# A two-layer diffusion backbone: weight splits moved from GpSimd and VectorE to VectorE and ScalarE, the second layer's shift and scale as packed matmuls

## The chip, the cores and the metric

The kernel runs on one core of a Trainium2 chip. The metric is the device time of one execution in microseconds; the time given for a kernel is the median of its timed runs. TensorE's clock has two levels, 1.2 and 2.4 GHz; the profile gives the mean of what was granted in a stretch as a fraction of the full one.

## What is computed

Two layers over 512 latent and 256 context tokens, width 2048, float32. Each layer: RMS norm, shift and scale by a modulation vector, a token mixer, and a gated residual. Layer 0's mixer is a bidirectional gated linear recurrence (16 blocks of 128 channels), layer 1's is differential attention with 16 heads.

```python
for i in range(2):
    shift, scale, gate = split(silu(c) @ mod_w[i] + mod_b[i], 3)          # for latent; the same with c_ctx
    h = rms_norm(x, norm_g[i]) * (1 + scale) + shift                      # latent and context tokens
    if i == 0:
        u, g = split(h @ lru_w_in, 2)
        xc = depthwise_conv(u) + conv_b
        r, ig = sigmoid(block_matmul(xc, gate_w) + gate_b)                # per direction
        y = (scan_forward + scan_backward)(r, ig, xc) * silu(g) @ lru_w_out
    else:
        q, k, v, g = split(h @ att_w_in, 4)                               # q, k: norm and rotary positions
        o = (softmax(q1 @ k1.T) - lam * softmax(q2 @ k2.T)) @ v           # per head
        y = (rms_norm(o) * silu(g)) @ att_w_out
    x = x + gate * y
return x                                                                  # latent tokens
```

## The kernel before

Every large product runs as three matmuls in a reduced-precision float32 form: an operand is *split* into a high part (a cast) and the rest (a subtraction), and high x high, high x low and low x high are summed in PSUM. Weights come in units of 128 x 1024 (512 KB), loaded on SP's queue into two buffers `raw`, split by `weights` into `wh` and `wl` (five buffers each; in layer 1 every sixth unit goes to an extra one). `split` (lines 43 to 50) issues the cast on one engine (line 49, or 47 on ScalarE) and the subtraction on another (line 50). The default is a cast on VectorE and a subtraction on GpSimd; in the attention every second unit is subtracted on VectorE, and the first output columns of the attention are cast on ScalarE. A unit's `raw` buffer is free for the next load when both are done.

The program runs in stages. The *prologue* loads and transposes the tokens and computes layer 0's shift and scale from 64 units of `mod_w`: four k-tiles of 256 columns go as four matmuls with 32-column stationary operands into the four quarters of PSUM's partitions (line 295), and `mod_cols` adds the four quarters with a small matmul (line 148). The *projections* (`phase1`) run 32 half-blocks (`proj`: 96 matmuls of 384 columns, lines 327 to 331), less the three begun in the prologue; between them, for each of 16 blocks, `padded` and `lru_conv` (first tap on GpSimd, line 426, three on VectorE, line 428, then the split into xh and xl), `lru_block` (24 gate matmuls of 386 columns, lines 451 to 453, ScalarE's functions, VectorE's scans) and `lru_out`. All of it shares eight PSUM banks. Beside it runs `mod_stream`, layer 1's shift and scale: `proj` takes a step of it after each weight unit (64/42 on average, from the eleventh unit on). A step loads a unit of 512 KB and adds it on VectorE, four multiply-adds of 512 columns (line 102); every eighth step's sums go through 16 small matmuls (line 115). The *output product* (`phase2`) multiplies by `w_out` in four column chunks of 512 (lines 557 to 559, three matmuls for each of six token tiles and two k-tiles of a unit; the fourth chunk in two halves), beside it layer 0's gate by VectorE's multiply-adds (line 102) and one matmul with ones (line 522); behind the last chunk the rows are normed and transposed again (`h_evac`: a product on ScalarE, a split). The *attention* (`phase3`, `head`) has, for each head, projections of 256 columns (lines 692 to 694), and between them the scores, softmax and products of the head before; `qk_norm` takes the four rotary products of q and of k on GpSimd (line 715). `early_out` and `phase4` are the attention's output product.

The order on each engine is the compiler's: it simulates the program as written, and issues by priority what is ready in the simulation. The engines then run their lists in order. `issue_after` keeps an instruction behind a named one on its own engine; `mod_stream` uses it to keep its steps behind the last result of `lru_out` (`self.mark`).

Of the kernel before, what the change touches and what calls it, by code (L numbers as in the profile page):

```python
# [29 lines left out]
# the last head's attention and the units of the first output columns beside it ("."), in order:  # L30
# q: channels, s: scores, t: transposes, v: times v, o: back to rows, f: norm, y: output
# [5 lines left out]
class Kern:  # L37
# [5 lines left out]
    def split(self, raw, hi, lo, hi_eng, lo_eng):  # L43
        """raw (float32) == hi + lo, both float32r"""
        nc = self.nc
        if hi_eng is nc.scalar:
            nc.scalar.copy(hi, raw)  # L47
        else:
            hi_eng.tensor_copy(hi, raw)  # L49
        return lo_eng.tensor_tensor(lo, raw, hi.bitcast(F32), op=ALU.subtract)  # L50

    def weights(self, src, shape, hi_eng=None, lo_eng=None):
        """one weight unit [128, 1024] from DRAM, split in two"""
# [10 lines left out]
        self.split(raw, h, l, hi_eng or nc.vector, lo_eng or nc.gpsimd)  # L64
# [9 lines left out]
    def rsqrt(self, pool, v, n, pre, bufs=1):  # L74
        """v ** -0.5 of a small tile: a guess from the bits of v, then Newton's steps"""
# [12 lines left out]
    def mod_vec(self, ch, pool, nm, bufs=1):  # L88
        """512 columns of silu(c) @ mod_w: sums over the channel tiles, one per partition"""
# [18 lines left out]
    def mod_stream(self, pool, chunks):  # L108
        """shift and scale of layer 1: four channel tiles per chunk"""
        nc = self.nc  # L110
        def sums(ch, acc):
            ps = self.psum("mcol")
            for s in range(4):
                for m in range(2):
                    nc.tensor.matmul(ps[:, 4 * s + 2 * m:4 * s + 2 * m + 2], acc[m][:, 128 * s:128 * s + 128],
                                     self.ones[:, 0:2], start=True, stop=True)
            for s in range(4):
                self.mod_col(1, 4 * ch + s, ps[:, 4 * s:4 * s + 4:2])

        last = None  # L120
# [22 lines left out]
    def mod_cols(self, layer, part, ch):  # L143
        """sums of the partials, channel-major: [128 channels, (latent, context)] x 2"""
# [97 lines left out]
    def rows(self, t, unit):  # L242
        """rms rows of one token tile, transposed"""
# [30 lines left out]
    def pairs(self, pool, unit):  # L274
        """shift and scale of layer 0 for two channel tiles at a time; behind them, h of these
        tiles and their part of the first three half-blocks"""
# [9 lines left out]
        for n in range(65):  # L286
            p, ch = n // 8, n // 8 + 8 * (n // 4 % 2)
            if n < 64:
# [3 lines left out]
                w = unit().rearrange("p (k c) -> p k c", k=4)  # L292
                nc.sync.dma_start(w, a["mod_w"][ch, u])
                for j in range(4):
# [829 lines left out]
```

## Time and profile before

| | |
|---|---|
| timed runs (median of 3) | 2505.36 us (2503.09 to 2505.61) |
| span of the profiled execution | 2499.5 us |
| TensorE busy, matmuls | 2350.4 us (94%), 15744 |
| TensorE busy, weight loads | 2197.3 us (88%) |
| VectorE busy | 1875.8 us (75%), 3292 instructions |
| ScalarE busy | 858.5 us (34%), 1826 |
| GpSimd busy | 694.9 us (28%), 390 |
| loads and stores | 298.83 MB, mean 120 GB/s |

The span runs from the first to the last instruction of one profiled execution; the timed runs take in what lies around it. In the rows below PE is TensorE (PEld its weight loads), DVE VectorE, ACT ScalarE, POOL GpSimd and SP the queue that issues most loads; L50 is line 50 of the code. Matmuls are pipelined, so TensorE's busy time is the time in which at least one was under way, and the pitch is read from the starts of successive ones. A float32 matmul that isn't in the reduced form leaves two records.

### The profile page before, as it was taken

What the parts mean: (1) busy time and instruction counts of PE and PEld (TensorE: products, weight loads), DVE (VectorE), ACT (ScalarE), POOL (GpSimd) and SP (SyncE); (2) the same over time, 40 slices, a digit from 0 to 9 for tenths busy, and PEclk for the clock granted to TensorE, in tenths of its full rate; (3) what the DMA queues carried; (4) which work ended last, traced back from release to release, by engine and by line L of the source; (5) the groups of instructions that cost most, each with busy time, mean ns of one, the idle gap of its engine ahead of it and who ended that gap; (6) DMA issues with size and microseconds to landing.
All of it is one profiled execution on the core that took longest, in us unless ns stands there. A gap on an engine that the chain in (4) does not pass through costs nothing.

```text
span 2499.5 us, 39647 instructions
## 1 busy us (share of the span) xinstructions
PE 2350.4 (94%) x15744; PEld 2197.3 (88%) x15744; DVE 1875.8 (75%) x3292; ACT 858.5 (34%) x1826; POOL 694.9 (28%) x390
## 2 busy tenths in 40 slices
PE   5989998989889899799999999999999999998899
PEld 4679998989889788679999999999999999997687
DVE  6457999999997866786787777778677766767622
ACT  4346535435337100033333333333333333235400
POOL 1243343433332233333121111212121211211352
PEclk8999999999999999999999999999999999999999
DMA  9912344434333655431232232322222211213552
GB/s 355 364 60 89 125 127 135 133 125 135 129 122 108 232 191 176 144 119 58 70 97 65 89 98 62 92 81 85 89 81 89 80 52 57 68 43 115 181 184 76
DMA packets 106473, 298.83 MB, mean 120 GB/s; under 512 B 12320, under 2 KB 33072, under 8 KB 106288
## 3 DMA queue, kind: packets, MB, share of 16 engines
q1 hardware_dynamic: 101536, 287.33, 35.2%
q10 hardware_dynamic: 4752, 8.98, 1.0%
q8 instruction: 123, 2.02, 0.3%
q14 instruction: 62, 0.51, 0.1%
HBM read 277.45 MB, written 18.82 MB: 119 GB/s over the span
## 4 chain that ended last, share of the span: by engine, by line
PE 42%; DVE 9%; DMA 3%; issue 2%; ACT 1%; POOL 1%; SPq 0%; DVEq 0%; ACTq 0%; POOLq 0%
PE pj L694 9%; PE pj L693 9%; PE pj L692 9%; PE sc L755 3%; PE acc L557 2%; DVE wh L49 2%; PE acc L558 2%; PE acc L559 2%; PE atr L778 1%; DMA raw<-w_kv 1%; DVE wl L50 1%; DMA raw<-w_o 1%; PE o L792 1%; PE o L791 1%; PE o L790 1%
## 5 line engine op out<-in xcount | busy, mean ns | idle before, releaser
L50 POOL TENSOR_TENSOR wl<-raw,wh 128x1024 fp32r<-128x1024 f32 x202 | 533.8, 2643 | 1334.8 <-DVE wh L49 975.1
L692 PE MATMUL pj<-wh,h 128*128 128x256 f32 x2560 | 730.2, 285 | 3.3 <-DVE v L50 2.7
L694 PE MATMUL pj<-wh,h 128*128 128x256 f32 x2560 | 729.2, 285 | 0.2
L693 PE MATMUL pj<-wl,h 128*128 128x256 f32 x2560 | 729.1, 285 | 0.0
L692 PEld LDWEIGHTS pj<-wh,h 128*128 128x128 f32 x2560 | 489.9, 191 | 6.2 <-DVE v L50 2.9
L693 PEld LDWEIGHTS pj<-wl,h 128*128 128x128 f32 x2560 | 490.2, 192 | 4.5 <-issue 2.6
L694 PEld LDWEIGHTS pj<-wh,h 128*128 128x128 f32 x2560 | 490.2, 191 | 3.1 <-issue 0.4
L49 DVE CAST wh<-raw 128x1024 fp32r<-128x1024 f32 x256 | 212.6, 832 | 173.4 <-PE acc L559 82.0
L102 DVE SCALAR_TENSOR_TENSOR ma<-mw,scT,ma 128x512 f32<-128x512 f32 x360 | 310.5, 906 | 18.9 <-DMA mw<-mod_v 18.9
L327 PE MATMUL proj<-h,wh 128*128 128x384 f32 x1024 | 265.5, 340 | 6.9 <-DVE h L49 6.9
L329 PE MATMUL proj<-h,wh 128*128 128x384 f32 x1024 | 271.6, 337 | 0.0
L331 PE MATMUL proj<-h,wl 128*128 128x384 f32 x1024 | 270.4, 336 | 0.0
L327 PEld LDWEIGHTS proj<-h,wh 128*128 128x128 f32 x1024 | 185.5, 190 | 15.2 <-DVE h L49 11.1
L329 PEld LDWEIGHTS proj<-h,wh 128*128 128x128 f32 x1024 | 187.2, 189 | 4.2 <-issue 2.0
L331 PEld LDWEIGHTS proj<-h,wl 128*128 128x128 f32 x1024 | 186.9, 189 | 0.8 <-issue 0.8
L761 ACT ACTIVATE p<-sc,mx 128x768 f32<-128x768 f32 x128 | 114.5, 904 | 113.1 <-DVE mx L757 108.1
L557 PE MATMUL acc<-wh,h 128*128 128x512 f32 x384 | 152.4, 398 | 0.0
L757 DVE TENSOR_REDUCE mx<-sc 128x2 f32<-128x1536 f32 x64 | 112.1, 1752 | 52.5 <-PE sc L755 52.3
L558 PE MATMUL acc<-wl,h 128*128 128x512 f32 x384 | 150.4, 392 | 0.1
L559 PE MATMUL acc<-wh,h 128*128 128x512 f32 x384 | 149.8, 391 | 0.0
L47 ACT CAST athl<-atr 128x512 fp32r<-128x512 f32 (+1 forms) x128 | 55.7, 483 | 196.7 <-PE atr L778 196.5
L755 PE MATMUL sc<-k,q 128*128 128x512 f32 (+1 forms) x512 | 108.2, 339 | 2.5 <-ACT p L761 2.5
(241 smaller groups left out, 3942.8 us busy)
## 6 DMA issues: line engine op xcount, KB each, us to landing
mw<-mod_v SPq DMA_DIRECT2D x96, 512.0 KB, 3.8
mw<-mod_w SPq DMA_DIRECT2D x64, 512.0 KB, 9.8
raw<-w_in SPq DMA_DIRECT2D x64, 512.0 KB, 3.6
raw<-w_kv SPq DMA_DIRECT2D x64, 512.0 KB, 3.7
raw<-w_qg SPq DMA_DIRECT2D x64, 512.0 KB, 3.9
raw<-w_out SPq DMA_DIRECT2D x40, 512.0 KB, 4.3
raw<-w_o SPq DMA_DIRECT2D x40, 512.0 KB, 3.5
raw<-mod_v SPq DMA_DIRECT2D x64, 256.0 KB, 3.6
```

Source lines behind the costliest of these rows:

```text
L49: hi_eng.tensor_copy(hi, raw)
L50: return lo_eng.tensor_tensor(lo, raw, hi.bitcast(F32), op=ALU.subtract)
L102: nc.vector.scalar_tensor_tensor(acc[m], w[:, k, :], sc, acc[m], op0=ALU.mult, op1=ALU.add)
L327: nc.tensor.matmul(ps[g][:, :384], wh, h[g][:, 0, :], start=first, stop=False)
L329: nc.tensor.matmul(ps[g][:, :384], wh, h[g][:, 1, :], start=False, stop=False)
L331: nc.tensor.matmul(ps[g][:, :384], wl, h[g][:, 0, :], start=False, stop=last)
L557: nc.tensor.matmul(acc[t], yh, wh, start=(kt == first), stop=False)
L558: nc.tensor.matmul(acc[t], yh, wl, start=False, stop=False)
L559: nc.tensor.matmul(acc[t], yl, wh, start=False, stop=(kt == last))
L692: nc.tensor.matmul(ps, h[:, 0, c], wh, start=(kt == 0), stop=False)
L693: nc.tensor.matmul(ps, h[:, 0, c], wl, start=False, stop=False)
L694: nc.tensor.matmul(ps, h[:, 1, c], wh, start=False, stop=(kt == KT - 1))
```

## The change

`weights` has no choice of engines any more: every weight unit is cast on ScalarE and subtracted on VectorE. The gate weights of `lru_block` go the same way; the first tap of the convolution goes to ScalarE; the subtractions of `h_evac` and the rotary products of `qk_norm` go to VectorE. What stays on GpSimd are clearings and, once, the tables of the rotary positions.

Layer 1's shift and scale are computed as layer 0's were: 16 chunks of four units, four packed matmuls for each unit, a copy of the partial sums on ScalarE and `mod_cols`. A step of `mod_stream` multiplies the unit loaded one step earlier and issues the next one's load, with no `issue_after`. The number of loads (64 of 512 KB) is unchanged, and so are the steps' places in `proj`. The host's layout of `mod_w` and `mod_v` follows, as do the chunk numbers in `mod_gate` and `gate_rows`.

```diff
-    def weights(self, src, shape, hi_eng=None, lo_eng=None):
+    def weights(self, src, shape):
...
-        self.split(raw, h, l, hi_eng or nc.vector, lo_eng or nc.gpsimd)
+        self.split(raw, h, l, nc.scalar, nc.vector)
...
-    def mod_stream(self, pool, chunks):
...
-        for ch in chunks:
-            g = self.mod_vec(4 + ch, pool, 2, 2)
-            for u in range(8):
-                with self.tc.issue_after(self.mark.ins) if self.mark else nullcontext():
-                    next(g)
-                yield
-                if u == 3 and last:
-                    sums(*last)
-            last = ch, self.macc
-        sums(*last)
+    def mod_unit(self, layer, ch, u, mps, w):
+        for j in range(4):
+            self.nc.tensor.matmul(mps[32 * j:32 * j + 32, :256], self.scp[:, 4 * u + j, :], w[:, j, :],
+                                  start=(u == 0), stop=(u == 3), tile_position=(0, 32 * j))
+    def mod_load(self, layer, ch, u, w):
+        w = w.rearrange("p (k c) -> p k c", k=4)
+        self.nc.sync.dma_start(w, self.a["mod_w"][layer, ch, u])
+        return w
+    def mod_part(self, mps, pool):
+        part = pool.tile([128, 256], F32, tag="mpart", bufs=2, name="mpart")
+        self.nc.scalar.copy(part, mps[:, :256])
+        return part
+    def mod_stream(self, pool):
+        unit = lambda n: self.mod_load(1, n // 4, n % 4, pool.tile([128, 1024], F32, tag="mw", bufs=2, name="mw"))
+        w, sums = unit(0), None
+        yield
+        for n in range(64):
+            ch, u = n // 4, n % 4
+            if u == 0:
+                mps = self.psum("mps")
+            self.mod_unit(1, ch, u, mps, w)
+            if n < 63:
+                w = unit(n + 1)
+            if u == 1 and sums:
+                self.mod_cols(1, *sums)
+            if u == 3:
+                sums = self.mod_part(mps, pool), ch
+            yield
+        self.mod_cols(1, *sums)
...
-        self.split(t, h[:, 0, :], h[:, 1, :], nc.vector, nc.gpsimd if g and kt % 2 == 0 else nc.vector)
+        self.split(t, h[:, 0, :], h[:, 1, :], nc.vector, nc.vector)
...
-        nc.gpsimd.tensor_scalar(xc, u[:, 2:2 + UL], cw[:, b, 2:3], self.convb[:, b:b + 1], op0=ALU.mult, op1=ALU.add)
+        nc.scalar.activation(xc, u[:, 2:2 + UL], AF.Identity, scale=cw[:, b, 2:3], bias=self.convb[:, b:b + 1])
...
-            self.split(raw, *self.gates, nc.vector, nc.gpsimd)
+            self.split(raw, *self.gates, nc.scalar, nc.vector)
...
-                nc.gpsimd.tensor_tensor(tv[:, :, c, :, h, :], xv[:, 0:4, c, :, 1 - h, :], sv[:, :, :, h, :], op=ALU.mult)
+                nc.vector.tensor_tensor(tv[:, :, c, :, h, :], xv[:, 0:4, c, :, 1 - h, :], sv[:, :, :, h, :], op=ALU.mult)
```

## Rows read from the trace of the kernel before

**Rows 1.** Table of stretches: busy us and instructions (x) per engine, clock, load share

```profile
150.00:802.00 652.00, 595.27 (x3306) 587.83 (x3305) 599.26 (x697) 322.57 (x434) 246.07 (x97) 0.95 0.37 121
802.00:1118.00 316.00, 292.60 (x1312) 238.32 (x1311) 245.85 (x329) 48.14 (x101) 106.59 (x41) 0.96 0.54 174
1118.00:2270.00 1152.00, 1132.52 (x9206) 1112.24 (x9205) 849.03 (x1784) 383.44 (x1069) 235.32 (x194) 1.00 0.24 75
2270.00:2420.00 150.00, 136.09 (x647) 110.56 (x646) 87.24 (x159) 47.24 (x103) 53.86 (x26) 0.95 0.54 174
2420.00:2499.50 79.50, 74.60 (x330) 61.43 (x328) 18.77 (x25) 0.00 (x0) 23.88 (x10) 0.98 0.28 89
```

**Rows 2.** Timeline, TensorE, projections: start us, us, instructions merged

```profile
480.56 0.51 PE L327 MATMUL proj<-h,wh 128*128 128x384 f32 x2
...
481.60 0.51 PE L327 MATMUL proj<-h,wh 128*128 128x384 f32 x2
```

**Rows 3.** Table of stretches, by tile: PE, PEld and others of proj; mcol; ma

```profile
150.00:802.00 652.00, 494.47 (x2793) 487.69 (x2791) 15.19 (x30) 27.97 (x78) 0.95 0.37 121
150.00:802.00 652.00, 14.73 (x128) 15.40 (x128) 5.12 (x32) 0.95 0.37 121
150.00:802.00 652.00, 14.73 (x128) 15.40 (x128) 211.11 (x256) 0.95 0.37 121
```

**Rows 4.** TensorE's waits in the projections: us in total, times, longest

```profile
PE gps L451 <- DVE xh L49: 32.1, 9, 7.8
PE gps L452 <- DVE xl L50: 17.0, 12, 2.5
PE gps L451 <- DVE ab L141: 3.8, 1, 3.8
PE gps L451 <- ACT r L455: 3.8, 1, 3.8
```

**Rows 5.** TensorE's waits in the output product, longest

```profile
PE gps L522 <- DVE ma L102: 20.0, 2, 13.2
```

**Rows 6.** Groups by form, whole span: busy us, mean ns, idle before, releaser

```profile
L50 POOL TENSOR_TENSOR wl<-raw,wh 128x1024 fp32r<-128x1024 f32 x202 | 533.8, 2643 | 1334.8 <-DVE wh L49 975.1 <-DVE l L762 72.6 <-ACT wh L47 47.4
L102 DVE SCALAR_TENSOR_TENSOR ma<-mw,scT,ma 128x512 f32<-128x512 f32 x360 | 310.5, 906 | 18.9 <-DMA mw<-mod_v 18.9
L49 DVE CAST wh<-raw 128x1024 fp32r<-128x1024 f32 x256 | 212.6, 832 | 173.4 <-PE acc L559 82.0 <-DMA raw<-w_o 25.6 <-DMA raw<-w_qg 25.0
L50 DVE TENSOR_TENSOR wl<-raw,wh 128x1024 fp32r<-128x1024 f32 x70 | 100.2, 1431 | 7.1 <-ACT wh L47 6.1
L1007 DVE SCALAR_TENSOR_TENSOR g<-g,pj 128x128 f32<-128x128 f32 x64 | 18.0, 282 | 10.6 <-ACT g L1006 9.9
L47 ACT CAST wh<-raw 128x1024 fp32r<-128x1024 f32 x16 | 16.8, 1050 | 16.9 <-DMA raw<-w_o 15.4 <-POOL rt L715 1.4
```

**Rows 7.** Timelines of VectorE and GpSimd, four places, in order of time

```profile
565.59 5.38 DVE L102 SCALAR_TENSOR_TENSOR ma<-mw,scT,ma 128x512 f32<-128x512 f32 x8
...
1051.12 6.13 POOL L50 TENSOR_TENSOR wl<-raw,wh 128x1024 fp32r<-128x1024 f32 x2 [4.54 <-DVE wh L49]
1052.94 6.18 DVE L102 SCALAR_TENSOR_TENSOR ma<-mw,scT,ma 128x512 f32<-128x512 f32 x4 [0.63 <-DMA mw<-mod_v]
...
2309.20 1.22 DVE L50 TENSOR_TENSOR wl<-raw,wh 128x1024 fp32r<-128x1024 f32 x1
```

**Rows 8.** Timeline, TensorE, prologue: packed products and small sums between projections

```profile
100.77 1.50 PE L295 MATMUL mps<-mw,scp 128*32 128x256 f32 x24
...
106.28 0.34 PE L331 MATMUL proj<-h,wl 128*128 128x384 f32 x1
106.55 0.64 PE L295 MATMUL mps<-mw,scp 128*32 128x256 f32 x8
107.12 0.98 PE L327 MATMUL proj<-h,wh 128*128 128x384 f32 x4
...
111.18 0.50 PE L148 MATMUL mcol<-sel,mpart 128*128 128x2 f32 x4
111.54 0.60 PE L327 MATMUL proj<-h,wh 128*128 128x384 f32 x2
```

More of the change, by code (lines that the diff above doesn't have):

```diff
@@ L106, in mod_vec @@
         yield
-    def mod_stream(self, pool, chunks):
[L110 to L120, printed above, removed]
-        for ch in chunks:
-            g = self.mod_vec(4 + ch, pool, 2, 2)
-            for u in range(8):
-                with self.tc.issue_after(self.mark.ins) if self.mark else nullcontext():
-                    next(g)
-                yield
-                if u == 3 and last:
-                    sums(*last)
-            last = ch, self.macc
-        sums(*last)
+    def mod_unit(self, layer, ch, u, mps, w):
[27 more added lines that the diff above has]
+        self.mod_cols(1, *sums)
     def mod_col(self, layer, c, src):
@@ L291, in pairs @@
                     mps = self.psum("mps")
-                w = unit().rearrange("p (k c) -> p k c", k=4)
-                nc.sync.dma_start(w, a["mod_w"][ch, u])
-                for j in range(4):
-                    nc.tensor.matmul(mps[32 * j:32 * j + 32, :256], self.scp[:, 4 * u + j, :], w[:, j, :],
-                                     start=(u == 0), stop=(u == 3), tile_position=(0, 32 * j))
+                self.mod_unit(0, ch, u, mps, self.mod_load(0, ch, u, unit()))
                 if n % 32 == 4:
@@ L314, in pairs @@
             if n % 4 == 3:
-                part = pool.tile([128, 256], F32, tag="mpart", bufs=2, name="mpart")
-                nc.scalar.copy(part, mps[:, :256])
-                sums = part, ch
+                sums = self.mod_part(mps, pool), ch
         for t in todo:
@@ L353, in phase1 @@
                 nc.gpsimd.memset(x, 0.0)
-            self.stream, self.slots = self.mod_stream(pool, range(8)), -16
+            self.stream, self.slots = self.mod_stream(pool), -16
             gates = lambda b: self.lru_block(b, x[b], pool)
@@ L516, in mod_gate @@
         nc = self.nc
-        yield from self.mod_vec(12 * layer + n, pool, nm)
+        yield from self.mod_vec(n, pool, nm)
         gt = self.gt[n] = pool.tile([128, nm, 512], F32, tag="gt", bufs=gbufs, name="gt")
@@ L534, in gate_rows @@
                 for i in range(2):
[L535 removed]
+                    nc.sync.dma_start(w[:, i], a["mod_v"][4 + n // 2, u + i][:, :, c])
                 for k in range(4):
@@ L875, in early_out @@
                     self.yload(u)
-                w = self.weights(a["w_o"][0, u], (2, 512), nc.scalar, nc.vector if u % 2 else None)
+                w = self.weights(a["w_o"][0, u], (2, 512))
                 with self.tc.issue_after(self.after.ins) if self.after else nullcontext():
@@ L958, in head @@
             return None
-        w = [self.weights(a["w_kv"][hd, u], (4, 256), None, nc.vector if u % 2 and hd else None) for u in range(4)]
+        w = [self.weights(a["w_kv"][hd, u], (4, 256)) for u in range(4)]
         if first:
@@ L1001, in head @@
         st["so"] = pa.tile([128, 4], F32, tag="so", bufs=2, name="so")
-        w = [self.weights(a["w_qg"][hd, u], (4, 256), None, nc.vector if u % 2 else None) for u in range(4)]
+        w = [self.weights(a["w_qg"][hd, u], (4, 256)) for u in range(4)]
         for t in range(4):
@@ L1073, in layout @@
     o["cT"] = c(np.stack([f["c"][0], f["c_ctx"]], -1).reshape(16, 128, 2).transpose(1, 0, 2))
-    o["mod_w"] = c(f["mod_w"][0, :, :4096].reshape(4, 4, 128, 16, 256).transpose(3, 0, 2, 1, 4))
-    v = f["mod_w"].transpose(1, 0, 2).reshape(2048, 12288)[:, 4096:]
-    o["mod_v"] = c(v.reshape(8, 2, 128, 16, 512).transpose(3, 0, 2, 1, 4))
+    o["mod_w"] = c(f["mod_w"][:, :, :4096].reshape(2, 4, 4, 128, 16, 256).transpose(0, 4, 1, 3, 2, 5))
+    v = f["mod_w"][:, :, 4096:].transpose(1, 0, 2).reshape(2048, 4096)
+    o["mod_v"] = c(v.reshape(8, 2, 128, 8, 512).transpose(3, 0, 2, 1, 4))
     o["mod_bT"] = c(f["mod_b"][:, :4096].reshape(2, 32, 128).transpose(2, 0, 1))
```

1 line of the change is left out of this document (removed).

## The prediction

> **What bounds the kernel now.** I cut the span where the work changes and read each stretch by the table of stretches [rows 1]: the prologue (0 to 150 us), the projections of layer 0 (150 to 802), their output product (802 to 1118), the attention heads (1118 to 2270) and the last output product. TensorE is busy everywhere, so the question in each stretch is what TensorE would need by itself, and who holds it up for the rest.
>
> In the projections VectorE is busy 599.26 of 652 us and TensorE 595.27 [rows 1]. TensorE's own need comes from its pitch at full clock: six 384-column matmuls start in 1.04 us (480.56 to 481.60), 0.1735 us each [rows 2]. 2793 projection matmuls lie in the stretch [rows 3]; the 16 x 24 gate matmuls of the code have 386 columns, so 0.1744 us each; the 128 small sums take 14.7 us [rows 3]: 484.6 + 67.0 + 14.7 = 566 us. So 86 of 652 us are lost: 56.7 idle (652 - 595.27), the rest in slices at 1.2 GHz, which the mean granted clock of 0.95 shows [rows 1]. The list of waits names the cause: 49.1 us of that idle time are gate matmuls waiting for VectorE's split of the convolution (xh, xl) [rows 4]. VectorE is the limit of this stretch, and TensorE stands close behind it.
>
> In the output product TensorE misses 23.4 us (316 - 292.60), 20.0 of them in two waits for the last multiply-add of the gate [rows 1, 5]; the clock then falls to its lower level. In the attention only 19.5 of 1152 us are idle at clock 1.00 [rows 1]: TensorE is the bound there and nothing this change touches can give much. After 2270 it misses 13.9 + 4.9 us.
>
> GpSimd's part is in the same rows. One of its splits takes 2643 ns on average [rows 6], and VectorE instructions that meet one grow: eight multiply-adds take 5.38 us (0.67 each) where it rests, but four take 6.18 us beside two GpSimd splits of 6.13 us [rows 7]. On average a multiply-add takes 906 ns [rows 6].
>
> **The change, part by part.** (1) *The second layer's shift and scale.* 256 VectorE operations (211.1 us in the projections [rows 3]) go, and 128 small sums on TensorE (14.7 us [rows 3]). In come 64 units of 4 packed products (8 records each). One between two projections moved the next one from 106.28 + 0.17 to 107.12, so it costs 0.67 us [rows 8]; three in a row take 1.50 us, 0.50 each [rows 8]. I take 0.67, as the stream hands out about one unit per weight unit: 64 x 0.67 = 43 us, bounds 32 to 43 at full clock, 86 if all fell into slices at half clock. The sums are now 16 groups of 4 small matmuls, each holding TensorE for 0.36 us (111.18 to 111.54 [rows 8]): 6 us. Sixteen copies on ScalarE lie beside. Net on TensorE: 43 + 6 - 14.7 = +34 us.
>
> The Trainium skill (TensorEngine Tiling (Array Packing), Key Properties) says that changing the tiling mode drains the TensorE. The row bears this out in kind, as a lone unit costs 0.17 us more than one in a row; if every unit cost only what one in a row does, the sum would be 11 us lower.
>
> The 64 loads stay as many and as large (512 KB). They are no longer placed behind the mixer's mark; each is issued on SP's queue right after the unit before it, some 8 us ahead of its use. A late load used to delay VectorE; now it would block TensorE, with all projections queued behind. I cost that at nothing, because TensorE's list of waits in this stretch has two more entries of 3.8 us each and neither is a load; the bounds are 0 and the 18.9 us that VectorE's multiply-adds of both streams waited for such loads [rows 6].
>
> (2) *The splits.* All 256 weight casts on VectorE (832 ns [rows 6]) go to ScalarE, where the 16 casts already there took 1050 ns [rows 6]; the 202 subtractions on GpSimd go to VectorE at 1431 ns as measured among GpSimd's, or 1.22 us alone [rows 6, 7]. In the projections that is 58 units (and 8 gate weights): VectorE loses 55 us and gains 66 x 1.22 = 81; ScalarE gains 66 x 1.05 = 69 us, and at most 16 x 1.05 = 17 for the convolution's first tap, which has fewer columns. VectorE there: 599 - 211 - 55 + 81 = 414 us before any relief from GpSimd's disappearance; ScalarE: 323 + 69 + 17 and 16 small copies, each shorter than such a cast (at most 17), = 426. Both are far below TensorE's need.
>
> (3) *Projections, sum.* TensorE needs 566 + 34 = 600 us. VectorE at 414 no longer holds the gates back, so the 49 us of waits and most of the low-clock slices behind them go. What is late next is ScalarE (table loads, gate functions and now the casts in one queue) and the eight PSUM banks, of which one is now held by a running sum for four units. I leave 12 us for these: 612 against 652, -40 us. Bounds: -50 (hardly anything left over) to -10 (loads and banks hold TensorE).
>
> (4) *Output product.* 40 casts leave VectorE (33 us at the mean), 40 subtractions come (49 us alone), 8 subtractions of h (384 columns) as well, its 128 multiply-adds stay. From 1052.94 to 1059.12 four of them took 6.18 instead of 2.7 us [rows 7], right ahead of the end of the 13.2 us wait [rows 5]. Each of the two GpSimd splits there cost VectorE about (6.18 - 2.7) / 2 = 1.7 us; for the eight weight units of that half chunk that is 14 us, and the dearer subtractions give 8 x (1.22 - 0.83) = 3 back. So some 10 of the 13 us go, the other wait (6.8 us) likewise in half, and with them the low-clock time: -20 us, bounds -30 to 0.
>
> (5) *Attention.* Per head VectorE loses 8 casts (6.7 us), gains about 4 subtractions (4.9) and 8 rotary products of 128 columns, at about 282 ns, the row of like size [rows 6] (2.3 us): even. ScalarE gains 8 x 1.05 = 8.4 us in about 72. These stand in queues that carry the softmax: a cast ahead of an exponential delays the transposes behind it by up to 1.05 us. TensorE has projection matmuls beside, placed by the compiler's schedule, and ScalarE's share goes from 383/1152 to about 517/1152 [rows 1]. I cost it at 0, bounds -10 (half the idle time) to +40 (2.5 us per head, two of eight casts exposed and one subtraction part-way).
>
> (6) *Ends.* In the last output product the chain load, cast, split shortens by 2.64 - 1.22 = 1.4 us [rows 6, 7] at each unit that GpSimd split, though ScalarE's cast is 0.2 slower: -5 us, bounds -10 to +2. The prologue's own work stays, and its six weight units have over 100 us of its loads to hide in: 0, bounds +-3.
>
> **How the numbers follow.** -40 - 20 + 0 - 5 = -65 us. The profiled span is 2499.5 us; the median of the three timed runs, 2505.36, stands 5.9 us above it, and I carry that over: 2499.5 - 65 + 5.9 = 2440 us.
>
> **Rivals.** *More is freed*: the waits of all stages go (-50, -30, -10, -10): 2405 us. For it: VectorE's waits alone explain most of TensorE's idle time. Against: each stage has a second limit close by. 0.14.
>
> *TensorE waits for the stream*: loads, banks or ScalarE's copies hold it in the projections, (3) gives -15 and the rest as forecast or a little less: 2465 to 2480. For it: SP's queue is one line, shared by weights whose buffers now wait for two busy engines. 0.18.
>
> *Slower, by the attention*: casts and subtractions stand ahead of the softmax on ScalarE and VectorE, and TensorE, which now idles 19.5 us, waits in every head. It decides once more than 65 us are lost there, 4.1 us per head out of the 13.3 us moved into these queues; at 6 us per head, 2536 us. Against: VectorE's load is even and ScalarE stays under half. 0.09.
>
> *It does not do what it says, or cancels*: the schedule packs differently and the 34 us of added TensorE time eat what the waits return in the projections (0), the attention loses what the output product wins: about 2502 us. 0.04.
>
> Forecast 0.55. The range 2408 to 2484 leaves out about half of the best case and the two worst, 0.2 in all. About 0.2% (5 us) is what a measurement of this kernel can tell from no change; faster 0.87, same 0.04, slower 0.09.
>
> **What would show it.** After: no GpSimd splits; VectorE near 60% in the projections; the multiply-adds of the gate near 0.67 us each; the waits for xh and xl gone; about 43 us of packed products between projections; the projections ending near 762 instead of 802; the wait of the gate's product under 5 us; an idle time in the attention still near 20 us. It would be wrong if TensorE's waits for the stream's loads or for ScalarE's evacuations exceed 25 us in the projections, or if the attention stretch grows beyond 1190 us.

## The result, and the profile of the kernel after

The kernel after takes 2441.84 us (median of 4 runs, 2437.47 to 2446.85), the kernel before, timed beside it, 2505.49 us: a ratio of 0.9748, 95% interval 0.9731 to 0.9765. The forecast was 2440 us. The profiled execution took 2444.69 us with a span of 2442.9, against a span of 2499.5 before. The stages below come from one execution of each kernel: their spans differ by 56.6 us, the medians by 63.7, so a stage is known to a few us only.

To compare stages I cut each run at TensorE's own landmarks: the first matmul of the output product, the first and the last projection matmul of the attention, the end. (The prediction's round cuts [rows 1] lie up to 12 us from these.)

| us | until the output product | output product | attention | rest | span |
|---|---|---|---|---|---|
| before | 801.8 | 304.7 | 1174.7 | 218.3 | 2499.5 |
| after | 774.8 | 292.3 | 1151.4 | 224.4 | 2442.9 |
| difference | -27.0 | -12.4 | -23.3 | +6.1 | -56.6 |
| forecast | -40 | -20 | 0 | -5 | -65 |

The table of stretches of the kernel after, from 150 us on. The columns are those of [rows 1]: stretch, length, then busy us (instructions) of PE, PEld, DVE, ACT and POOL, granted clock, DMA share, GB/s.

```profile
150.00:774.80 624.80, 611.22 (x3757) 577.33 (x3756) 351.33 (x440) 418.87 (x542) 5.01 (x12) 0.99 0.37 126
774.80:1067.10 292.30, 280.06 (x1219) 226.56 (x1218) 200.39 (x303) 87.96 (x135) 0.00 (x0) 0.97 0.53 182
1067.10:2218.50 1151.40, 1149.96 (x9394) 1132.87 (x9393) 780.24 (x1894) 513.80 (x1216) 0.00 (x0) 1.00 0.24 78
2218.50:2442.90 224.40, 201.32 (x881) 162.34 (x879) 106.62 (x181) 67.37 (x111) 0.00 (x0) 0.95 0.43 143
```

The same of the kernel before at the same landmarks, for the two stretches read most below:

```profile
150.00:801.80 651.80, 595.07 (x3305) 587.63 (x3304) 599.06 (x697) 322.37 (x434) 246.07 (x97) 0.95 0.37 121
1106.50:2281.20 1174.70, 1155.21 (x9394) 1134.94 (x9395) 864.95 (x1832) 391.31 (x1093) 237.72 (x195) 1.00 0.24 76
```

Subtract the first number behind the length from the length: TensorE's idle time in the projections fell from 56.7 to 13.6 us while its busy time rose from 595 to 611. In the attention the idle time fell from 19.5 to 1.4 us, which is 18 of the 23 us won there. VectorE went from 599 to 351 us in the projections, and from 865 to 780 in the attention, although it had got more instructions there (1894 for 1832).

TensorE's waits in the projections (us in total, times, longest), which answer to [rows 4]; there is no xh or xl any more, and no wait for a load:

```profile
PE mcol L159 <- ACT mpart L121: 5.1, 1, 5.1
PE gps L456 <- ACT r L460: 5.0, 1, 5.0
PE gps L456 <- ACT i L462: 3.5, 1, 3.5
```

In the output product, against [rows 5], and the longest one behind the attention, where before had none like it:

```profile
PE gps L527 <- DVE ma L102: 12.2, 2, 8.4
...
PE atr L783 <- DVE p L770: 6.4, 1, 6.4
```

TensorE's timeline around one packed unit (start us, us, merged records), against [rows 8]:

```profile
558.34 0.51 PE L336 MATMUL proj<-h,wl 128*128 128x384 f32 x2
558.78 0.64 PE L111 MATMUL mps<-mw,scp 128*32 128x256 f32 x8
559.35 0.62 PE L332 MATMUL proj<-h,wh 128*128 128x384 f32 x2
```

Two projection matmuls from 558.34 at a pitch of 0.1735 [rows 2] would let the next start at 558.69; it started at 559.35, 0.66 us later. The unit's price is the 0.67 of the prediction. Read in the same way, the 16 units that stand alone between projections cost 0.66 to 0.67 us each; ten times two units stand together, and a pair costs 1.10 us, so its second unit 0.44.

The groups that answer to [rows 6], whole span for the splits, the output product for the multiply-adds (busy us, mean ns, idle before and releaser); then the multiply-adds of the kernel before in its output product, and four in a row in the timeline of the kernel after:

```profile
L47 ACT CAST wh<-raw 128x1024 fp32r<-128x1024 f32 x272 | 285.0, 1051 | 483.6 <-PE acc L564 186.3
L50 DVE TENSOR_TENSOR wl<-raw,wh 128x1024 fp32r<-128x1024 f32 x272 | 331.5, 1222 | 248.8 <-ACT wh L47 248.1
...
L102 DVE SCALAR_TENSOR_TENSOR ma<-mw,scT,ma 128x512 f32<-128x512 f32 x120 | 83.2, 747 | 10.6 <-DMA mw<-mod_v 10.5
```

```profile
L102 DVE SCALAR_TENSOR_TENSOR ma<-mw,scT,ma 128x512 f32<-128x512 f32 x120 | 108.4, 954 | 7.7 <-DMA mw<-mod_v 7.7
```

```profile
1002.00 2.73 DVE L102 SCALAR_TENSOR_TENSOR ma<-mw,scT,ma 128x512 f32<-128x512 f32 x4
```

A subtraction takes 1222 ns on average now, and a multiply-add of this stretch 747 instead of 954 ns (the 906 of [rows 6] is the mean of the whole span). Successive records overlap, so four in a row take 2.73 us, 0.68 each.

### The profile page after: what moved, and what is told of

Its sections match the earlier page's. It is cut to its first block, busy times and chain, and to the rows that moved or that the text cites. A ratio compares the mean times of both kernels' runs of the same rounds, so it can differ in the third digit from the quotient of the medians.

```text
span 2442.9 us, 40114 instructions
## 1 busy us (share of the span) xinstructions
PE 2363.8 (97%) x16192; PEld 2187.5 (90%) x16192; DVE 1514.2 (62%) x3126; ACT 1152.8 (47%) x2131; POOL 7.3 (0%) x20
## 3 DMA queue, kind: packets, MB, share of 16 engines
q1 hardware_dynamic: 101536, 287.33, 34.7%
## 4 chain that ended last, share of the span: by engine, by line
PE 85%; ACT 5%; DVE 5%; DMA 4%; issue 1%; SPq 0%; ACTq 0%; DVEq 0%
PE pj L699 12%; PE pj L698 12%; PE pj L697 12%; PE proj L332 7%; PE proj L334 7%; PE proj L336 7%; PE acc L562 4%; PE acc L563 4%; PE acc L564 4%; PE sc L760 4%; PE mps L111 3%; PE atr L783 2%; DMA raw<-w_o 1%; DVE wl L50 1%; PE o L796 1%
## 5 line engine op out<-in xcount | busy, mean ns | idle before, releaser
L47 ACT CAST wh<-raw 128x1024 fp32r<-128x1024 f32 x272 | 285.0, 1051 | 483.6 <-PE acc L564 186.3
L50 DVE TENSOR_TENSOR wl<-raw,wh 128x1024 fp32r<-128x1024 f32 x272 | 331.5, 1222 | 248.8 <-ACT wh L47 248.1
L563 PE MATMUL acc<-wl,y 128*128 128x512 f32 x256 | 101.7, 397 | 3.4 <-DVE wl L50 3.4
```

What stands on the lines that cost most here:

```text
L563: nc.tensor.matmul(acc[t], yh, wl, start=False, stop=False)
```

## Experiments: which half of the change did it

The change has two halves that can stand alone. Theory from the prediction: the stream's removal of 211 us from VectorE ends the waits in the projections, and pays for its own TensorE time. Rival: GpSimd's leaving relieves VectorE enough by itself.

**stream_only**: the change with the splits, the first tap and the rotary products left on the engines of before.

```diff
-        self.split(raw, h, l, nc.scalar, nc.vector)
+        self.split(raw, h, l, hi_eng or nc.vector, lo_eng or nc.gpsimd)
```

> The kernel before with the packed stream of layer 1's shift and scale alone; all splits, the convolution's tap and the rotary products stay where they were. Limit theory (VectorE's sum of work held the projections): VectorE loses 211 us of 599 there, so the waits for xh and xl fall from 49 us to under 10, TensorE's need of about 600 us decides, and the first matmul of the output product comes at 778 to 788 us instead of 801.8; the later stages keep their lengths (output product 304.7, attention 1174.9). Time about 2485 us. Rival (GpSimd's collisions and its slow first tap held the gates, not VectorE's sum): the waits stay above 25 us, the first output matmul comes at 800 or later, since TensorE also has 34 us more to do; time 2505 us or more.

**splits_only**: the kernel before with the change's engines, and VectorE's multiply-adds kept for the second layer's shift and scale.

```diff
-        self.split(raw, h, l, hi_eng or nc.vector, lo_eng or nc.gpsimd)
+        self.split(raw, h, l, nc.scalar, nc.vector)
...
-                nc.gpsimd.tensor_tensor(tv[:, :, c, :, h, :], xv[:, 0:4, c, :, 1 - h, :], sv[:, :, :, h, :], op=ALU.mult)
+                nc.vector.tensor_tensor(tv[:, :, c, :, h, :], xv[:, 0:4, c, :, 1 - h, :], sv[:, :, :, h, :], op=ALU.mult)
```

> The kernel before with everything of the change but the packed stream: splits on ScalarE and VectorE, the tap on ScalarE, rotary products on VectorE; layer 1's shift and scale stay VectorE's multiply-adds. Limit theory: VectorE in the projections has 599 - 55 + 81 = 625 us less what the collisions cost; if that is under 80 us it still holds TensorE, the first output matmul stays at 790 to 805 us, and the gain is that of the later stages as the changed kernel shows it (output product -12, attention -23, end +6): about 2475 us. Rival (the collisions were the cause, the sum was not): VectorE falls to about 500 us there, the waits for xh and xl go, TensorE needs 34 us less than with the stream, the first output matmul comes at 770 or earlier and the time is 2445 us or less.

Measured: stream_only 2476.08 us, ratio 0.9883 (0.9868 to 0.9898); splits_only 2404.01 us, ratio 0.9598 (0.9582 to 0.9614). Half of the change is 38 us faster than the whole. The projections end (first output matmul) at 777.3 and 728.7, against 801.8 before and 774.8 after: -24.5 and -73.1 alone, -27.0 together. The stretch up to there in the table of stretches, of stream_only and then of splits_only, the waits for xh and xl that are left in stream_only, and the longest of TensorE's waits in splits_only:

```profile
150.00:777.30 627.30, 611.45 (x3749) 576.38 (x3748) 392.41 (x441) 351.67 (x471) 211.81 (x96) 0.99 0.37 126
```

```profile
150.00:728.70 578.70, 571.77 (x3302) 570.79 (x3301) 502.95 (x693) 412.01 (x525) 6.10 (x12) 0.99 0.43 136
```

```profile
PE gps L457 <- DVE xl L50: 3.8, 2, 2.2
PE gps L456 <- DVE xh L49: 2.8, 2, 2.0
```

```profile
PE gps L451 <- ACT r L455: 3.5, 1, 3.5
PE gps L451 <- ACT i L457: 3.5, 1, 3.5
```

In splits_only VectorE keeps all 256 operations of the stream, is busy 503 of 579 us, and TensorE still never waits for it. Each half by itself ends most or all of VectorE's hold on the gates (xh and xl together: 49.1 us before, 6.6 in stream_only, none in splits_only). The second half to come finds little or nothing left to free, and the stream then only adds its TensorE time: 774.8 - 728.7 = 46.1 us, of which 39.4 are busy time (611.22 - 571.77) and 6.7 idle. In rotary_back and att_sub_back (below), which share the kernel after's code up to here, the stretch ends at 771.0 and 768.5 us with TensorE busy 607.72 and 606.43 us: the stream costs 40 to 46 us, 35 to 39 of them busy time.

**pool_idle_work**: is it GpSimd's presence that slows VectorE, or the work it hands over? splits_only, with 46 subtractions added on GpSimd during the projections that read a weight unit and write a tile that nobody reads; VectorE's own work is that of splits_only.

```diff
+            if s > 8:
+                high = w[0].rearrange("p k c -> p (k c)").bitcast(F32)
+                self.nc.gpsimd.tensor_tensor(self.waste, high, high, op=ALU.subtract)
```

> The kernel splits_only with one more GpSimd subtraction of 128x1024 beside each of the last 46 weight units of the projections; it reads the high part twice and writes to a tile that nobody reads, so no result waits for it. It measures what GpSimd's mere work costs VectorE. Theory P (the two engines lock each other out for whole instructions): VectorE's busy time in the projections grows by 46 x 1.0 to 1.7 = 46 to 80 us from 503, the 772-column operations from about 0.95 us back towards 1.1 to 1.3, waits for xh and xl return, and the first output matmul comes at 745 to 775 instead of 728.7; time 2420 to 2450 us. Rival (what was slow before was the wait for GpSimd's results, not its presence): VectorE grows by less than 15 us, the first output matmul stays at 728 to 733, time 2404 us.

Measured: 2463.18 us (0.9843, 0.9827 to 0.9858), 59 us slower than splits_only. The stretch of the projections in pool_idle_work, TensorE's two longest waits there, and three groups (two of VectorE from 250 us on, GpSimd's own); then the two VectorE groups of splits_only:

```profile
150.00:785.00 635.00, 593.66 (x3309) 586.96 (x3308) 573.64 (x696) 413.39 (x526) 113.66 (x58) 0.96 0.37 124
```

```profile
PE gps L454 <- DVE xh L49: 27.2, 10, 5.2
PE gps L455 <- DVE xl L50: 6.9, 9, 1.5
```

```profile
L102 DVE SCALAR_TENSOR_TENSOR ma<-mw,scT,ma 128x512 f32<-128x512 f32 x239 | 213.5, 934 | 2.7 <-DMA mw<-mod_v 2.5
L431 DVE SCALAR_TENSOR_TENSOR xc<-up,conv_wT,xc 128x772 f32<-128x772 f32 x36 | 42.6, 1183 | 0.0
L339 POOL TENSOR_TENSOR tab<-wh 128x1024 f32<-128x1024 f32 x46 | 108.3, 2354 | 427.4 <-ACT wh L47 427.3
```

```profile
L102 DVE SCALAR_TENSOR_TENSOR ma<-mw,scT,ma 128x512 f32<-128x512 f32 x237 | 166.6, 744 | 3.0 <-DMA mw<-mod_v 2.9
L428 DVE SCALAR_TENSOR_TENSOR xc<-up,conv_wT,xc 128x772 f32<-128x772 f32 x36 | 36.3, 1007 | 0.0
```

The same VectorE instructions cost 573.64 instead of 502.95 us: 70.7 us for 46 GpSimd operations, 1.54 us of VectorE for each operation of 2.35 us. The waits for xh and xl are back, the clock is back at 0.96, and 56 of the 73 us that the splits had won in the projections are gone. The profile names no instruction that waited for the added ones. So the presence alone does it. The view of a single line (shortest/median/longest ns, first and last start) shows how, for the multiply-adds and the casts xh of pool_idle_work, then for the multiply-adds of splits_only:

```profile
L102 DVE SCALAR_TENSOR_TENSOR ma<-mw,scT,ma x240: 718/744/2402, 248.9 to 734.6; 128x512 f32<-128x512 f32 x120
L49 DVE CAST xh<-xc x16: 531/550/2211, 166.1 to 759.5; 128x772 fp32r<-128x772 f32 x16
```

```profile
L102 DVE SCALAR_TENSOR_TENSOR ma<-mw,scT,ma x240: 712/744/753, 247.5 to 678.4; 128x512 f32<-128x512 f32 x120
```

The median is the same; some instructions are hit, and the longest takes 1.65 us more, while the added GpSimd operations take 1.89 us at their shortest. The Trainium skill (SBUF — State Buffer, section Who interferes with whom) says that a VectorE instruction with two SBUF inputs contends with a GpSimd instruction that reads SBUF, that a cast can contend as well, and that the ports they share are an exclusive lock. This run agrees in kind: the two groups shown grew (744 to 934 ns, 1007 to 1183) and read two SBUF tensors, and the cast xh, with one input, grew too (551 to 653 ns on average). The 1.54 us of 2.35 is a mean over operations that met VectorE at any point of their length.

**splits_cast_dve**: is it the casts' move to ScalarE instead? splits_only with every cast of `weights` on VectorE, so that GpSimd rests and ScalarE is spared (the eight casts of the gate weights stay on ScalarE).

```diff
-        self.split(raw, h, l, nc.scalar, nc.vector)
+        self.split(raw, h, l, nc.vector, nc.vector)
```

> The kernel splits_only with all weight casts on VectorE (the subtractions stay there too), read stage by stage against splits_only. Attention, theory C (the 128 casts in VectorE's queue, each waiting for its load or a free buffer in front of the softmax's steps, made the idle time): TensorE's idle time rises from 1 to 12 to 20 us and the attention from 1152 to 1165 to 1175 us. Theory D (no single one of the three moves, GpSimd's absence as a whole): it stays at 1149 to 1157. Projections: VectorE 503 + 66 x 0.69 = 549 us of 579, so the gates begin to wait again and the first output matmul comes at 732 to 750 instead of 728.7; if ScalarE's queue were the later one, at 722 to 728. End (from the last attention projection): 224.5 -> 218 if the exponentials that stood behind casts waiting for loads made the 6 us wait, 224 or more if the loads themselves did. Time 2420 us by C, 2402 by D.

Measured: 2412.85 us (0.964, 0.9626 to 0.9654); projections until 745.6, attention 1151.5. With VectorE at 535.61 of 595.6 us, the gates waited 0.9 us for xh; 14.3 us were one wait at the stream's end (TensorE's two longest waits):

```profile
PE mcol L115 <- DVE ma L102: 14.3, 1, 14.3
PE gps L451 <- ACT r L455: 3.2, 1, 3.2
```

So the casts' move is worth 17 of the 73 us in the projections, most of it that one wait, and nothing in the attention.

**unit_twice**: the packed unit's price. The kernel after, with four packed products by zeros added to each of the 64 units.

```diff
-                                  start=(u == 0), stop=(u == 3), tile_position=(0, 32 * j))
+                                  start=(u == 0), stop=(u == 3 and not layer), tile_position=(0, 32 * j))
+        if layer:
+            for j in range(4):
+                self.nc.tensor.matmul(mps[32 * j:32 * j + 32, :256], self.zero, w[:, j, :],
+                                      start=False, stop=(u == 3), tile_position=(0, 32 * j))
```

> The changed kernel with the four packed products of each of layer 1's 64 units followed by four more with a stationary operand of zeros into the same sums (they add nothing). It measures what a packed unit costs next to another. If TensorE is the limit of the projections: 64 x 0.45 to 0.50 = 29 to 32 us, the first output matmul at 800 to 808 instead of 775, time about 2472 us. Rival (ScalarE's queue sets the pace and the products lie in TensorE's gaps): under 10 us. Rival (the packed shape lowers the clock or drains on every unit): over 40 us.

Measured: 2475.58 us (0.9889, 0.9872 to 0.9905). The projections end 23.3 us later than after's (0.36 us for each added unit), TensorE is 25.8 us busier (0.40), the median is 33.7 us higher (0.53). Against rotary_back and att_sub_back the projections end 27.1 and 29.6 us later, and 6.4 us of the whole difference lie in the output product (298.7 against 292.3), which the edit does not touch. The stretch of the projections:

```profile
150.00:798.10 648.10, 637.01 (x4262) 592.23 (x4261) 350.88 (x437) 417.79 (x541) 5.94 (x12) 0.99 0.36 121
```

TensorE time added to this stretch lengthens it nearly one for one, so it is TensorE that bounds it, and a second unit in a row is cheaper than the first (0.66), as in the pairs above (0.44). The Trainium skill (TensorEngine Tiling (Array Packing), Key Properties), with its drain at a change of mode, agrees in kind.

## Experiments: the attention

The attention lost 23.3 us, and the forecast was 0. Three things had left GpSimd and VectorE there: the rotary products, half the subtractions, and the casts.

**rotary_back**: the kernel after with the rotary products on GpSimd.

```diff
-                nc.vector.tensor_tensor(tv[:, :, c, :, h, :], xv[:, 0:4, c, :, 1 - h, :], sv[:, :, :, h, :], op=ALU.mult)
+                nc.gpsimd.tensor_tensor(tv[:, :, c, :, h, :], xv[:, 0:4, c, :, 1 - h, :], sv[:, :, :, h, :], op=ALU.mult)
```

> The changed kernel with the eight rotary products of each head back on GpSimd. Theory A (the attention's 23 us came from the q chain, which no longer waits for GpSimd between the norm and the transposes): half of it or more comes back, attention from the first to the last projection matmul 1151.7 -> 1163 to 1172, time about 2455 us. Theory B (it came from the weight splits, whose subtraction on GpSimd locked VectorE for 2.5 us at a time in front of the softmax): the attention stays within 1149 to 1157 us and the time within 5 us of the changed kernel's.

**att_sub_back**: the kernel after with every second weight subtraction of the attention on GpSimd.

```diff
-        w = [self.weights(a["w_kv"][hd, u], (4, 256)) for u in range(4)]
+        w = [self.weights(a["w_kv"][hd, u], (4, 256), nc.vector if u % 2 else nc.gpsimd) for u in range(4)]
```

(the same for `w_qg`)

> The changed kernel with the subtraction of every second weight unit of the attention back on GpSimd (casts stay on ScalarE, rotary products on VectorE). Theory A (q chain): the attention stays at 1149 to 1157 us. Theory B (GpSimd's long subtractions lock VectorE): VectorE's instructions grow again (the 768-column multiply-add from about 1.0 to about 1.3 us on average), TensorE's idle time in the attention returns from 1 us to 10 or more, the attention takes 1162 to 1175 us and the kernel about 2455 us.

Measured: 2442.33 us (0.9748, 0.9733 to 0.9762) and 2444.53 us (0.9756, 0.9735 to 0.9777), attention 1151.0 and 1152.8: neither brings anything back.

**att_both_back**: both at once, on splits_only.

```diff
-                nc.vector.tensor_tensor(tv[:, :, c, :, h, :], xv[:, 0:4, c, :, 1 - h, :], sv[:, :, :, h, :], op=ALU.mult)
+                nc.gpsimd.tensor_tensor(tv[:, :, c, :, h, :], xv[:, 0:4, c, :, 1 - h, :], sv[:, :, :, h, :], op=ALU.mult)
...
-        w = [self.weights(a["w_qg"][hd, u], (4, 256)) for u in range(4)]
+        w = [self.weights(a["w_qg"][hd, u], (4, 256), nc.vector if u % 2 else nc.gpsimd) for u in range(4)]
```

> The kernel splits_only with both of the attention's GpSimd parts back, the rotary products and every second unit's subtraction; the casts stay on ScalarE. Theory F (one GpSimd queue in which rotary products stand behind subtractions of 2.6 us, and both lock VectorE): TensorE's idle time in the attention rises from 1 to 8 us or more, the attention from 1152 to 1160 to 1172 us, time about 2415 us. Rival (it takes the casts in VectorE's queue as well, any two of the three leave enough room): the attention stays at 1149 to 1157 us.

Measured: 2413.84 us (0.9645, 0.9629 to 0.9661), attention 1155.4 against splits_only's 1152.1; the rest of the loss is in the output product (303.9 against 296.2). The first head's weights reach into it, but it also took 302.0 us in splits_early_dve (below), which changes nothing there, so the reason is not shown. Not it either.

**att_weights_back**: what is left is the casts on VectorE together with GpSimd's subtractions, on splits_only; the rotary products stay on VectorE.

```diff
-        w = [self.weights(a["w_qg"][hd, u], (4, 256)) for u in range(4)]
+        w = [self.weights(a["w_qg"][hd, u], (4, 256), nc.vector, nc.vector if u % 2 else nc.gpsimd) for u in range(4)]
```

(`w_kv` likewise, with all of the first head's `w_kv` subtractions on GpSimd, in this run and in att_both_back)

> The kernel splits_only with the attention's weight splits as they were (casts on VectorE, the subtraction of every second unit on GpSimd), while the rotary products stay on VectorE. Casts alone, subtractions alone, rotary products alone, and subtractions with rotary products left the attention within 1151 to 1155 us. Theory G (a cast and the subtraction behind it on the two engines that lock each other out, 64 times): idle time 8 us or more, the attention at 1160 to 1175 us, time about 2418 us. Rival (only all three together fill VectorE's and GpSimd's queues so that TensorE waits): at 1149 to 1157 us.

Measured: 2427.77 us (0.9705, 0.9689 to 0.9722), attention 1175.4: in the profiled execution, all of the loss comes back from this pair. That execution took 2436.27 us; if all of its 8.5 us above the median of the four lay in the attention, 15 of the 23 us would be left, still far from the 1151.0 to 1155.4 of the other experiments on the attention. The attention in the table of stretches, TensorE's two longest waits in it and two VectorE groups of att_weights_back, then the same of splits_cast_dve (casts alone on VectorE), then two groups of att_sub_back (subtractions alone on GpSimd):

```profile
1036.90:2212.30 1175.40, 1159.72 (x9394) 1139.48 (x9395) 864.77 (x1947) 389.56 (x1086) 152.72 (x61) 0.99 0.23 75
```

```profile
PE atr L778 <- DVE qvk L707: 8.0, 4, 3.3
PE otr L826 <- DVE ot L819: 4.3, 5, 1.4
```

```profile
L49 DVE CAST wh<-raw 128x1024 fp32r<-128x1024 f32 x122 | 116.2, 953 | 48.8 <-DMA raw<-w_qg 18.6 <-DMA raw<-w_kv 14.5 <-PE pj L694 12.0
L765 DVE SCALAR_TENSOR_TENSOR p<-p,l 128x768 f32<-128x768 f32 x60 | 74.4, 1240 | 0.4
```

```profile
1039.20:2190.70 1151.50, 1149.43 (x9392) 1132.59 (x9391) 859.10 (x2014) 390.16 (x1089) 0.00 (x0) 1.00 0.25 78
```

```profile
L49 DVE CAST wh<-raw 128x1024 fp32r<-128x1024 f32 x125 | 86.2, 689 | 44.2 <-PE pj L694 19.0 <-DMA raw<-w_qg 13.7 <-DMA raw<-w_kv 7.2
L765 DVE SCALAR_TENSOR_TENSOR p<-p,l 128x768 f32<-128x768 f32 x60 | 60.9, 1016 | 0.7
```

```profile
L50 DVE TENSOR_TENSOR wl<-raw,wh 128x1024 fp32r<-128x1024 f32 x63 | 105.9, 1681 | 68.7 <-ACT wh L47 68.4 <-issue 0.3
...
L770 DVE SCALAR_TENSOR_TENSOR p<-p,l 128x768 f32<-128x768 f32 x60 | 62.9, 1049 | 0.6
```

VectorE is as busy in splits_cast_dve (859 us) as in att_weights_back (865), and its attention is 24 us shorter in these executions: the load is not what counts. What differs is which instruction meets GpSimd. When VectorE makes the cast, GpSimd starts behind it while VectorE goes on with the next head's casts and the softmax; the casts grow from 689 to 953 ns and the combination of the softmax (p) from 1016 to 1240. When ScalarE makes the cast, VectorE's weight subtraction grows to 1681 ns, for which TensorE does not wait, and p is at 1049. TensorE's waits in att_weights_back name neither the casts nor p, but other steps of VectorE's list (the norm of q and k, the output norm). So that the pair costs the time is shown; that it does so by this order is read from the groups, and no run changed the order alone.

## Experiments: the end and the output product

Behind the attention the change lost 6.1 us. VectorE's maximum of the last scores (mx) and ScalarE's timeline behind it in the kernel after:

```profile
2268.47 1.76 DVE L762 TENSOR_REDUCE mx<-sc 128x2 f32<-128x1536 f32 x1 [1.18 <-PE sc L760]
...
2276.17 1.05 ACT L47 CAST wh<-raw 128x1024 fp32r<-128x1024 f32 x1 [1.79 <-DMA raw<-w_o]
2278.67 1.04 ACT L47 CAST wh<-raw 128x1024 fp32r<-128x1024 f32 x1 [1.45 <-DMA raw<-w_o]
2279.62 0.37 ACT L47 CAST athl<-atr 128x256 fp32r<-128x256 f32 x1
2279.88 0.91 ACT L766 ACTIVATE p<-sc,mx 128x768 f32<-128x768 f32 x1
```

The exponentials at 2279.88 had their maximum by 2270.2 (2268.47 + 1.76), but stood behind other work of ScalarE's list, of which two casts waited 1.79 and 1.45 us for loads. TensorE waited 6.4 us for what follows.

**splits_early_dve** and **splits_early_pool**: splits_only with the 16 casts of the first output columns on VectorE, or on GpSimd.

```diff
-                w = self.weights(a["w_o"][0, u], (2, 512))
+                w = self.weights(a["w_o"][0, u], (2, 512), nc.vector)
```

(`nc.gpsimd` in the second)

> The kernel splits_only with the casts of the first output columns' weights (16 units beside the last head) on VectorE; all others stay on ScalarE. Theory E (on ScalarE a cast that waits for its load holds up the last head's exponentials behind it): the 6 us wait of the transposes for VectorE's difference goes, the low clock behind it too, and the end shrinks from 224.5 to 215 to 219 us: about 2397 us. Rival (two raw buffers and loads of 3 to 4.5 us set the pace whoever casts): the wait turns up at another matmul and the end stays at 222 to 227 us: 2404 us.

> As splits_early_dve, but these 16 casts on GpSimd, so that neither ScalarE nor VectorE stands behind a load for a cast (VectorE's subtraction still follows it). Theory E: the end is 214 to 219 us, 2396 us, if a cast on GpSimd takes under 2 us. Rival (pace of loads and buffers): each unit's chain grows by the slower cast, 1 to 2 us, the end is 228 us or more.

Measured: 2406.68 us (0.9612, 0.9598 to 0.9627) and 2403.21 us (0.96, 0.9585 to 0.9614), against 2404.01 of splits_only; the end takes 225.0, 220.6 and 224.5 us. TensorE's waits in it, of the first and then two of the second:

```profile
PE atr L778 <- DVE p L765: 5.2, 2, 5.1
```

```profile
PE acc L558 <- DVE wl L50: 11.5, 7, 3.1
...
PE atr L778 <- DVE p L765: 0.7, 1, 0.7
```

On VectorE the casts stand ahead of the softmax in that engine's list instead, and the wait stays (5.2 us; 6.2 in splits_only). On GpSimd, with nothing behind them, it is down to 0.7 us, but the weights now come late (11.5 us in seven waits for wl): the stretch is 3.9 us shorter, the time the same within the intervals. `raw` has two buffers, and a cast that waits for its load blocks whatever stands behind it on its engine; a third buffer was not tried.

**gate_ahead**: splits_early_pool, with the four chunks' gate sums of layer 0 as one sequence that runs ahead of the chunks (31 steps for 24 units, a second set of sum tiles).

```diff
-        yield from self.mod_vec(12 * layer + n, pool, nm)
+        yield from self.mod_vec(12 * layer + n, pool, nm, 2)
...
-            gate = self.mod_gate(0, 0, pool, 2)
+            gate = (None for n in range(4) for _ in self.mod_gate(0, n, pool, 2))
...
-                        next(gate, None)
+                        steps += 31 / 24
+                        while steps >= 0.999:
+                            next(gate, None)
+                            steps -= 1
...
```

> The kernel splits_early_pool with layer 0's gate sums running ahead: 31/24 of a step beside each weight unit of the first three column chunks, so that nearly nothing is left for the fourth, whose halves give VectorE only half the time per unit. If the wait of the gate's matmul (12 us of idle time and the low clock behind it) comes from VectorE's multiply-adds of the fourth chunk, it goes and the output product shrinks from 297 to 278 to 286 us; time about 2390 us. Rival (VectorE is then late in the earlier chunks or the loads are): the wait moves and the output product stays at 292 us or more.

Measured: 2398.9 us (2396.96 to 2401.75; 0.9584, 0.9565 to 0.9603), the lowest median here, 43 us below the kernel after, though its interval overlaps those of splits_only and splits_early_pool. The output product, which was to shrink to 278 to 286 us, went only from 296.9 to 295.1. TensorE's waits in it, and VectorE's timeline ahead of the second:

```profile
PE gps L522 <- DVE ma L102: 5.1, 1, 5.1
PE acc L557 <- DVE gt L523: 4.7, 1, 4.7
```

```profile
952.47 0.69 DVE L523 TENSOR_TENSOR gt<-gps,gt 128x512 f32<-128x512 f32 x1 [2.44 <-DMA gt<-mod_bg]
```

The wait for the sums fell (12.1 us in two waits in splits_early_pool) and a new one took its place, for the gate itself, whose addition had waited 2.44 us for the bias row's load.

## Why the prediction was right, and where it was not

The time (2441.8 for 2440) and the cause in general (VectorE frees the gates, GpSimd's collisions end) were right. The terms were not: three stages were forecast too good by 13, 8 and 11 us, one too bad by 23, and the span missed by 8 us (-56.6 for -65). That the total still came within 2 us is luck, twice: these errors cancelled in part, and the offset gave the rest. The median lay 5.9 us above the profiled span before, and lies 1.1 us below it after. Each later run is only about 2 us longer than its own span (2444.69 for 2442.9), so most of the 5.9 that I carried over was a profiled execution of before some 4 us below the median, not time around the span.

- **(1) The stream.** Its price held: 0.66 us for a lone unit, forecast 0.67; the whole stream costs 39.4 us of busy TensorE time given the splits, 36.0 and 34.7 in rotary_back and att_sub_back, forecast 34 net. The 128 sums and the groups of four that I counted are records: line 115 issues 8 matmuls for a chunk (not 16), `mod_cols` 2, and each leaves two records; the times hold. What failed is the account: the prediction treated it as what pays for the end of the waits. With the splits done it pays for nothing and costs 40 to 46 us of the projections, and no rival of mine said that a half of the change would beat the whole.
- **(2) The splits.** The failed step. I put VectorE at 414 us "before any relief from GpSimd's disappearance", named the relief and gave it no number. Without the stream's part that sum is 599 - 55 + 81 = 625 us; splits_only measured 503; the kernel after measured 351 for the 414. In splits_only the relief is 122 us, against 211 for the multiply-adds that I did count (by pool_idle_work's 70.7 us for 107.6 us of GpSimd's time, before's 246.07 us would have cost about 160, an estimate). Had it stood in the sum, it would have put VectorE, with all its multiply-adds kept, below TensorE's own need of 566 us, and the stream's worth in doubt. ScalarE was right (419 for 426). [Rows 7] held the price: (6.18 - 2.7) / 2 = 1.7 us for each GpSimd split, which I used for the output product only; pool_idle_work gave 1.54.
- **(3) Projections.** Of the waits I was right: xh and xl are gone. 12 us were to be left above TensorE's need of 600; measured 25 (624.8 against 600): 13.6 idle, all of it the three waits for ScalarE shown above, the rest not idle. ScalarE as the next limit was named, and undersized. No load of the stream ever held TensorE, so the rival that had it wait for the stream did not come.
- **(4) Output product.** -12.4 inside the bounds of -30 to 0. The multiply-adds fell to 0.68 us each in a row, 0.67 forecast, but the longest wait went from 13.2 to 8.4 us, not under 5. In VectorE's list the dearer subtractions (1222 ns) stand between them; that these are the reason was not tested. gate_ahead shows a second wait close behind.
- **(5) Attention.** -23.3, outside the bounds of -10 to +40. I counted instructions moved and found VectorE even. Its load did not matter (859 and 865 us for 1151.5 and 1175.4); the casts on VectorE beside GpSimd's subtractions did. "Nothing this change touches can give much" was wrong by the idle 18 us that I had read and left standing.
- **(6) Ends.** +6.1 instead of -5, outside the bounds of -10 to +2. The mechanism is the slower rival's, casts ahead of the softmax on ScalarE, but in the one place where they wait for loads, and at 6 us instead of more than 65.

One thing stays open: the kernels that share the stream's code for the projections reached the output product at 774.8, 771.0 and 768.5 us, and the kernel after's own runs spread over 9 us where splits_only's spread over 2.5. No run here tells why.

## What to carry to other kernels

When two parts of a change relieve the same engine, price each with the other already made: the second may free nothing and still cost what it adds to the engine that bounds. An engine's work off the critical path is not free if it slows another's instructions: take the price of a collision from one pair in the timeline and multiply it by the count, before moving any arithmetic. And work in an in-order queue that waits for a load belongs where nothing urgent stands behind it; here that took one wait away, and the time stayed within the noise.

## What the runs showed of the hardware

GpSimd work that nobody waits for cost VectorE 1.54 us for each 2.35 us operation. It did so by hitting some instructions hard (a multiply-add of 744 ns took up to 2402), not by slowing all. VectorE's reduction of the scores (mx), which reads PSUM, took 1752 ns beside GpSimd's subtractions in att_sub_back and 1755 without in splits_cast_dve, while a two-input SBUF instruction there grew by up to 38% (1222 to 1681 ns). A cast of 128 x 1024 took 1.04 us on GpSimd (median of splits_early_pool's 16, one took 2.06), 1.05 on ScalarE and 0.69 on VectorE: GpSimd's subtraction (1.89 us at its shortest and 2.35 on average in pool_idle_work) is the slow one, not its cast.
